# Conditioning products of a decoder step taken in batches: each tile loaded by a fixed pattern of granules, and two to four of them multiplied together behind a given projection matmul

## The chip, the cores and the metric

The kernel runs on one core of a Trainium2 chip. The metric is the device time of one execution in microseconds (us); three runs of the kernel before are known, and one profiled execution. The engines are called PE (matrix multiply), ACT, DVE and POOL (elementwise work); SP issues most of the DMAs, POOL and ACT some.

## The reference

One inference step of a decoder layer for 256 prompt tokens and 8 x 4 sample tokens, 288 columns in all, at a model width of 2048. Cut to what matters here:

```python
mod = jax.nn.silu(c) @ P['w_ada'] + P['b_ada']          # c: 9 rows; w_ada: 2048 x 12288
sh1, sc1, gt1, sh2, sc2, gt2 = split(mod, 6)
xn = rmsnorm(x, P['g_norm1']) * (1.0 + sc1) + sh1
mix, st = mixer(xn, ...)     # x @ w_in; RG-LRU, GLA and mLSTM branches; three gated merges; @ w_out
x = x + gt1 * mix
xn = rmsnorm(x, P['g_norm2']) * (1.0 + sc2) + sh2
x = x + gt2 * (jnp.square(jax.nn.relu(xn @ P['w_ff1'])) @ P['w_ff2'])
y = rmsnorm(x, g_final)
```

All values are 32-bit floats. The conditioning matrix `w_ada` alone is 100 MB, read once; it is multiplied with only nine rows (one prompt, eight samples).

## The kernel before, in words

**Projections.** Activations lie feature by feature: 16 tiles of 128 features by 288 columns. Weights come in granules: `stream` (L144) loads a granule of 256 rows by 512 columns (512 KB, L153), splits it into a rounded part `hi` on ACT (L154) and a rest `lo` on DVE (L155), and PE multiplies, for four blocks of 128 columns and two of 128 rows, `hi` with the high part of the activations, `hi` with their low part, and `lo` with the high part (L161 to L163). A granule is 24 matmuls. A projection over 2048 rows takes eight granules and ends with four evacuations (`evac`), each under high priority. Load and split are traced under high priority too, except in a few first blocks (`ahead`). The tiles `raw`, `hi` and `lo` have three buffers each; from the third merge on, `at` lets some of them use other memory in rotation (the tag `st`, which before holds recurrent states, and the slots 8 and 9).

**Conditioning.** `cond_product` (L204) multiplies the nine rows with one large matrix. A unit is a tile of 1 MB (768 KB in the correction product): one 128-row slice of 2048 columns, or two slices of 1024. Its four matmuls per slice (L216) go to the four 32-column parts of the PE array and add up in the PSUM tile `pa`. After 16 slices the sum is transposed and finished on DVE. The matrices follow in a fixed order: the two halves of SC1, then SH1, then the correction of the projections q, k, v for the shift ("cor", which reads `win` again), then GT1, SH2, SC2, GT2. From the second half of SC1 on this is the generator `fillers`. `run` asks it for one step after a granule as `pace["every"]` says: after each granule in the first blocks, then every second, two of three, every eighth. One step traces the load of a unit and its matmuls, at normal priority. `drain` runs the steps on until a given matrix is done. Each load gets its tile from `raw_tile`: the slots in `slots["ids"]` in turn (memory that lies free at the time), or the one ring tile `ag` (None). From the GLA branch on this is `ag` alone, until the output projection adds slots 8 and 9.

**Order.** The instructions are not executed in the order of the program text. A planner orders each engine's queue ahead of time, by a simulated timeline: among the instructions whose inputs and buffers it takes to be ready it picks by priority, which is the program's order, moved ahead for what stands under `tc.high_priority()`. Each engine then executes its queue in that order and waits where something is not there yet.

**Stages.** The first half of the scale, then q, k and half of v over the first and second halves of the features; the shift; the rest of v; two LRU blocks; the LRU branch; a small projection and the gates' two blocks; the GLA branch; the first merge, the mLSTM input and branch, the second and the third merge; the output projection; the second norm; then for eight blocks of the hidden layer `ff1` and `ff2`.

Of the kernel before, what the change touches and what calls it, by code (L numbers as in the profile page):

```python
# [8 lines left out]
F32 = mybir.dt.float32  # L9
# [19 lines left out]
CONSTS = [("ident", 128), ("eye", 32), ("bcol", 8), ("smask", 32), ("slo", 32), ("shi", 32),  # L29
          ("glo", 128), ("ghi", 128), ("causal", 128), ("bdm", 128), ("hsel", 4), ("seli", 128), ("self", 128), ("head", 4), ("half", 2)]  # L30
# [22 lines left out]
def trunk(ctx, tc, io):  # L53
# [92 lines left out]
    def stream(w, blk, act, kt, evac, g0=0, width=512, ahead=True, k0=0):  # L146
# [3 lines left out]
        for g in range(k0 // 2, kt // 2):  # L150
# [5 lines left out]
            for m in range(nm_t):  # L156
                for kk in range(2):
# [5 lines left out]
                    T.matmul(pss[m][:, :N], lo[:, kk, ms], xh, start=False, stop=k == kt - 1)  # L163
# [5 lines left out]
    pace = {"every": (), "n": 0}  # L169
# [26 lines left out]
    slots = {"ids": (None,), "n": 0}  # L196
# [8 lines left out]
    def cond_product(load, each, cols, stat, finish):  # L205


        ps = pa.tile([P, 512], F32, tag="pa", name=nm("pa"))
        for q in range(KT // each):
            raw = raw_tile()  # L210
            load(raw, q)
            for i in range(each):
                k = each * q + i
                v = raw[:, cols * i:cols * i + cols].rearrange("p (m j f) -> p j m f", j=4, f=32)
                for j in range(4):
                    T.matmul(ps[32 * j:32 * j + 32, 0:cols // 4], stat(k), v[:, j], start=k == 0, stop=k == KT - 1)  # L216
            if q < KT // each - 1:
                yield
        with tc.high_priority():
            for h in range(-(-cols // 1024)):  # L220
                finish(h, by_feature(ps, h, min(256, cols // 4 - 256 * h)))
        yield
# [15 lines left out]
    def ada(kind):  # L238
        def load(raw, k):
            Q.dma_start(raw.rearrange("p (h m) -> p h m", h=2), wada[kind, :, k].rearrange("h p m -> p h m"))  # L240
        return cond_product(load, 1, 2048, silu_c, ada_finish(kind))
# [1041 lines left out]
```

## Time and profile before

| | us |
|---|---|
| median of three runs | 2048.25 |
| lowest, highest | 2047.21, 2050.35 |
| the profiled execution | 2049.13 |
| its span, from the first to the last instruction | 2047.4 |
| PE busy | 1991.3 (97%) |
| DVE, ACT, POOL busy | 1030.3, 803.1, 304.0 |
| bytes moved by DMA | 429.69 MB, mean 210 GB/s |

The profile lists the instructions of that execution by line, engine and tiles, with their busy time and mean duration, and behind a bar the time that the engine stood idle before them and what ended it. The granted clock of PE is a share of full speed. PE's ends are modelled, since its matmuls are pipelined; so the starts of matmuls that follow one another are read rather than their durations.

### The profile page before, as it was taken

How to read it: one execution, taken by the hardware profiler on the slowest of the kernel's cores; microseconds unless marked ns; L12 is line 12 of the kernel's file. 1: busy time of each engine (PE TensorE's matmuls, PEld its weight loads, DVE VectorE, ACT ScalarE, POOL GpSimd, SP SyncE). 2: the span in 40 equal slices, each digit the busy share in tenths (PEclk: the TensorE clock that was granted, in tenths of full speed). 3: DMA queues.
4: the chain of work that ended last, by engine and by line, in shares of the span. 5: the costliest groups of instructions: out<-in, count | busy, mean ns of one | idle time of the engine just before them, and what ended most of it. 6: DMA issues, size and time to landing. Idle time of an engine off the chain costs nothing.

```text
span 2047.4 us, 35126 instructions
## 1 busy us (share of the span) xinstructions
PE 1991.3 (97%) x14726; PEld 1832.7 (90%) x14726; DVE 1030.3 (50%) x1410; ACT 803.1 (39%) x1099; POOL 304.0 (15%) x345
## 2 busy tenths in 40 slices
PE   6999999999999999999999999999999999999997
PEld 3778868987889798889998889999999999999997
DVE  4454556455554356464444464434454444454565
ACT  3323375332445332243333354444343434343434
POOL 0120112022212223100002241101010101010102
PEclk8989999999999999999999999999999999999999
DMA  9987686458673257877778655555555555555552
GB/s 389 349 317 249 220 311 210 157 201 294 220 242 127 89 196 243 260 263 266 249 238 328 221 174 165 166 166 165 168 166 165 166 168 164 167 165 165 165 165 98
DMA packets 121023, 429.69 MB, mean 210 GB/s; under 512 B 11601, under 2 KB 13809, under 8 KB 120737
## 3 DMA queue, kind: packets, MB, share of 16 engines
q1 hardware_dynamic: 111728, 393.59, 57.0%
q0 software_dynamic: 7984, 29.14, 3.9%
q10 hardware_dynamic: 1152, 4.72, 0.6%
q8 instruction: 115, 1.88, 0.4%
q14 instruction: 44, 0.35, 0.1%
HBM read 410.59 MB, written 16.81 MB: 209 GB/s over the span
## 4 chain that ended last, share of the span: by engine, by line
PE 89%; DMA 5%; DVE 3%; issue 2%; ACT 1%; POOL 1%; DVEq 0%; SPq 0%; POOLq 0%; ACTq 0%
PE mm L161 27%; PE mm L163 26%; PE mm L162 26%; PE pa L216 5%; DMA st<-mC 2%; DMA raw<-win 1%; DVE lo L155 1%; DMA s<-wada 1%; DMA o_C_s<-st 1%; ACT hi L154 0%; PE px L948 0%; PE pi L993 0%; PE px L675 0%; DMA st<-gla 0%; PE px L566 0%
## 5 line engine op out<-in xcount | busy, mean ns | idle before, releaser
L155 DVE TENSOR_TENSOR lo<-raw,hi 128x1024 fp32r<-128x1024 f32 (+1 forms) x424 | 541.3, 1279 | 596.6 <-ACT hi L154 580.0
L154 ACT ACTIVATE hi<-raw 128x1024 fp32r<-128x1024 f32 (+1 forms) x424 | 442.7, 1046 | 792.4 <-PE mm L162 677.7
L161 PE MATMUL mm<-xh,hi 128*128 128x288 f32 x2168 | 648.2, 301 | 10.1 <-ACT xh L341 5.5
L162 PE MATMUL mm<-xl,hi 128*128 128x288 f32 x2168 | 642.4, 297 | 1.2 <-DVE xl L342 1.2
L163 PE MATMUL mm<-xh,lo 128*128 128x288 f32 x2168 | 632.6, 297 | 3.5 <-DVE lo L155 3.5
L161 PEld LDWEIGHTS mm<-xh,hi 128*128 128x128 f32 x2168 | 408.1, 189 | 67.0 <-issue 40.0
L163 PEld LDWEIGHTS mm<-xh,lo 128*128 128x128 f32 x2168 | 405.9, 189 | 13.4 <-DVE lo L155 5.6
L162 PEld LDWEIGHTS mm<-xl,hi 128*128 128x128 f32 x2168 | 409.6, 189 | 3.2 <-DVE xl L342 1.5
L162 PE MATMUL mm<-s,hi 128*128 128x288 f32 x1176 | 349.0, 297 | 0.0
L161 PE MATMUL mm<-s,hi 128*128 128x288 f32 x1176 | 348.3, 298 | 0.0
L163 PE MATMUL mm<-s,lo 128*128 128x288 f32 x1176 | 345.9, 296 | 0.0
L161 PEld LDWEIGHTS mm<-s,hi 128*128 128x128 f32 x1176 | 220.6, 188 | 13.0 <-issue 10.9
L163 PEld LDWEIGHTS mm<-s,lo 128*128 128x128 f32 x1176 | 220.9, 188 | 1.8 <-issue 1.2
L162 PEld LDWEIGHTS mm<-s,hi 128*128 128x128 f32 x1176 | 221.3, 188 | 1.1 <-issue 0.4
L1121 POOL TENSOR_TENSOR t<-t 128x288 f32<-128x288 f32 x64 | 62.6, 990 | 639.6 <-ACT t L1120 639.6
L161 PE MATMUL mm<-s,st 128*128 128x288 f32 x488 | 143.9, 296 | 0.0
L162 PE MATMUL mm<-s,st 128*128 128x288 f32 x488 | 143.3, 294 | 0.0
L154 ACT ACTIVATE st<-s 128x1024 fp32r<-128x1024 f32 x80 | 84.8, 1060 | 135.6 <-PE mm L162 86.9
L161 PE MATMUL mm<-xh,st 128*128 128x288 f32 x408 | 120.7, 298 | 0.7 <-DVE xl L1107 0.7
L162 PE MATMUL mm<-xl,st 128*128 128x288 f32 x408 | 120.3, 296 | 0.0
L161 PEld LDWEIGHTS mm<-s,st 128*128 128x128 f32 x488 | 91.7, 188 | 0.8 <-ACT t L296 0.8
L162 PEld LDWEIGHTS mm<-s,st 128*128 128x128 f32 x488 | 91.9, 188 | 0.0
(373 smaller groups left out, 2113.7 us busy)
## 6 DMA issues: line engine op xcount, KB each, us to landing
raw<-win SPq DMA_DIRECT2D x192, 512.0 KB, 4.4
raw<-wf SPq DMA_DIRECT2D x176, 512.0 KB, 3.3
ag<-wada SPq DMA_DIRECT2D x57, 1024.0 KB, 5.9
s<-wf SPq DMA_DIRECT2D x80, 512.0 KB, 3.5
s<-wada SPq DMA_DIRECT2D x39, 1024.0 KB, 8.5
raw<-wout SPq DMA_DIRECT2D x32, 512.0 KB, 4.3
s<-win SPq DMA_DIRECT2D x11, 768.0 KB, 6.4
st<-mC POOLq DMA_DIRECT2D x16, 514.0 KB, 5.1
```

Of the source, the lines that this page charges most:

```text
L154: S.activation(hi, raw, AF.Copy)
L155: V.tensor_tensor(out=lo, in0=raw, in1=hi.bitcast(F32), op=ALU.subtract)
L161: T.matmul(pss[m][:, :N], hi[:, kk, ms], xh, start=k == k0, stop=False)
L162: T.matmul(pss[m][:, :N], hi[:, kk, ms], xl, start=False, stop=False)
L163: T.matmul(pss[m][:, :N], lo[:, kk, ms], xh, start=False, stop=k == kt - 1)
L216: T.matmul(ps[32 * j:32 * j + 32, 0:cols // 4], stat(k), v[:, j], start=k == 0, stop=k == KT - 1)
L1121: G.tensor_tensor(out=r, in0=r, in1=r, op=ALU.mult)
```

## The change

Load and product of a conditioning unit come apart. `cond_product` now yields units: a name, a function that takes a tile and issues its load, a function that multiplies it, and for the last unit of a matrix a function that finishes. A pattern of letters, one per granule, says what follows a granule: L loads the next unit (`load_one`, under high priority), V multiplies all units that are loaded and not yet multiplied, up to the end of a matrix (`visit`, under high priority, and on PE not ahead of the granule's last matmul), X does both. The patterns are X up to the shift; `LLLL.V` up to the LRU branch, with eight tiles in turn (slots 5, 6, 7, `ag`, 0, 1, 3, 4); nothing in the small projection; `LLLL.V..` in the gates; `LL.V..` and from its third block on `L.V...` in the first merge; nothing in the mLSTM input, the second merge and the output gate; `LLL.V..` in the third merge; `LLLL.V..` in the output projection; and in the feed-forward, from the second hidden block on, a pattern of 21 granules with three loads and one visit. Where tiles of the tag `st` hold a unit, two of them hold half a unit each, and the load is two DMAs.

Four things go with it. The split tiles `hi` and `lo` no longer use `st` and slot 9. Four constant tables (`shi`, `ghi`, `seli`, `self`, 416 columns) are gone: the upper clamps use the negated lower tables, and two selectors are made by POOL from the identity. The matmul that adds the new tokens' part to a sample state's output comes behind the products of the first states in place of ahead of them. And the three units that were asked for between the output projection and the second norm are no longer placed there. The first block of q is now loaded ahead like the others.

The diff, cut to its core:

```diff
-                    T.matmul(pss[m][:, :N], lo[:, kk, ms], xh, start=False, stop=k == kt - 1)
+                    pace["last"] = T.matmul(pss[m][:, :N], lo[:, kk, ms], xh, start=False, stop=k == kt - 1)
...
+    def every(p):
+        pace.update(every=p, n=0)
     def run(gen):
         for _ in gen:
-            pace["n"] += 1
-            e = pace["every"]
-            if e and e[pace["n"] % len(e)]:
-                next(fill, None)
+            if pace["every"]:
+                step(pace["every"][pace["n"] % len(pace["every"])])
+                pace["n"] += 1
...
     def raw_tile():
+        i = slots["ids"][slots["n"] % len(slots["ids"])]
         slots["n"] += 1
-        i = slots["ids"][slots["n"] % len(slots["ids"])]
         if i is None:
-            return ring.tile([P, 2048], F32, tag="ag", name=nm("ag"))
-        return flat(slot(i))[:, 0:2048]
+            return [ring.tile([P, 2048], F32, tag="ag", name=nm("ag"))]
+        if i == "st":
+            return [sp.tile([P, 1028], F32, tag="st", name=nm("st"), bufs=2)[:, 0:1024] for _ in range(2)]
+        return [flat(slot(i))[:, 0:2048]]
...
+                for h, r in enumerate(raw):
+                    v = r[:, w * i:w * i + w].rearrange("p (m j f) -> p j m f", j=4, f=32)
+                    for j in range(4):
+                        T.matmul(ps[32 * j:32 * j + 32, h * w // 4:(h + 1) * w // 4], stat(k), v[:, j], start=k == 0 and h == 0,
+                                 stop=k == KT - 1, skip_group_check=True)
...
+        for q in range(n):
+            def ld(q=q):
+                raw = raw_tile()
+                load(raw, q)
+                return raw
+            yield name, ld, lambda raw, q=q: products(raw, q), end if q == n - 1 else None
...
-    def fillers():
-        yield from ada_half(SC1, 1)
+    def units():
+        yield from ada_half("sc0", SC1, 0)
+        yield from ada_half("sc", SC1, 1)
...
+    def load_one():
+        u = next(left, None)
+        if u:
+            held.append((u[0], u[1](), u[2], u[3]))
+    def visit():
+        while held:
+            name, raw, products, end = held.pop(0)
+            products(raw)
+            if end:
+                end()
+                done.add(name)
+                return
+    def step(c):
+        if c in "LX":
+            with tc.high_priority():
+                load_one()
+        if c in "VX":
+            with tc.high_priority(), tc.issue_after(pace["last"].ins):
+                visit()
+    def settle():
+        while held:
+            visit()
     def drain(n):
         while n not in done:
-            next(fill, None)
+            if not held:
+                with tc.high_priority():
+                    load_one()
+            visit()
...
-    pace["every"] = (1,)
+    every("X")
     for b in range(NPRE):
-        run(stream(win, B_Q + b, act1, 8, to_slot((qk, vv)[b // 2], 4 * (b % 2)), ahead=b > 0))
+        run(stream(win, B_Q + b, act1, 8, to_slot((qk, vv)[b // 2], 4 * (b % 2))))
...
-    pace["every"] = (1, 0)
-    slots["ids"] = 6, 7, None
+    every("LLLL.V")
+    slots.update(ids=(5, 6, 7, None, 0, 1, 3, 4), n=0)
...
+    drain("cor")
+    settle()
+    every("")
...
+    every("LLLL.V..")
+    slots.update(ids=(6, 7, "st", None), n=0)
     run(stream(win, B_GATE, act1, KT, gate_silu(0)))
...
-            V.tensor_tensor(out=am[:, t], in0=am[:, t], in1=C("ghi").unsqueeze(1).to_broadcast(bc), op=ALU.min)
+            V.scalar_tensor_tensor(am[:, t], C("glo").unsqueeze(1).to_broadcast(bc), -1.0, am[:, t], ALU.mult, ALU.min)
...
-            T.matmul(po[0:32, 0:256], asb[:, h], vs[:, 0:256], start=True, stop=False, skip_group_check=True)
...
+                if q == 0:
+                    T.matmul(po[0:32, 0:256], asb[:, h], vs[:, 0:256], start=False, stop=False, skip_group_check=True)
...
-    drain("cor")
-    slots["ids"] = None,
+    settle()
     ygla = gla()
...
+            if br == 0 and b == 2:
+                settle()
+                slots.update(ids=(None,), n=0)
+                every("L.V...")
...
-    pace["every"] = (1, 0, 0)
+    slots.update(ids=(None, 7), n=0)
+    every("LL.V..")
     merge(0, ylru, io["wbl"])
+    settle()
+    every("")
...
-        def gate_rows(sel):
+        def gate_rows(i):
             p = misc()
-            T.matmul(p[:, :N], C(sel), sm, start=True, stop=True)
+            sel = t288()[:, 0:P]
+            G.tensor_copy(sel.rearrange("p (h i) -> p h i", h=4), ident.rearrange("p (h i) -> p h i", h=4)[:, :, i:i + 1].to_broadcast([P, 4, 32]))
+            T.matmul(p[:, :N], sel, sm, start=True, stop=True)
...
-    at.update(lo=(None, None, "st"), hi=(None, None, "st"))
+    slots.update(ids=(None, 5, "st"), n=0)
+    every("LLL.V..")
...
-    slots["ids"] = 8, 9, None
+    settle()
+    slots.update(ids=(8, 9, None, "st"), n=0)
+    every("LLLL.V..")
...
-    for _ in range(3):
-        next(fill, None)
...
-    at.update(raw=(None, None, 8), lo=(None, None, 9, None, None, "st"))
+    at.update(raw=(None, None, 8))
+    slots.update(ids=(9, None, "st"), n=0)
+    every("L..L..L.." + "...V" + 8 * ".")
     for hb in range(8):
-        pace["every"] = (1, 0, 0, 0, 0, 0, 0, 0)
         hn = ff1(hb + 1) if hb < 7 else None
         if hb == 6:
-            all_of(fill)
+            drain(GT2)
```

More of the change, by code (lines that the diff above doesn't have):

```diff
@@ L212, in cond_product, with products @@
+    def cond_product(name, load, each, cols, stat, finish):
+        acc_ = []
+        def products(raw, q):
+            if not acc_:
+                acc_.append(pa.tile([P, 512], F32, tag="pa", name=nm("pa")))
+            ps = acc_[0]
+            w = cols // len(raw)
             for i in range(each):
                 k = each * q + i
-                v = raw[:, cols * i:cols * i + cols].rearrange("p (m j f) -> p j m f", j=4, f=32)
-                for j in range(4):
-                    T.matmul(ps[32 * j:32 * j + 32, 0:cols // 4], stat(k), v[:, j], start=k == 0, stop=k == KT - 1)
@@ L984, in mlstm @@
             r = slice(32 * h, 32 * h + 32)
-            T.matmul(po[0:32, 0:257], psb[:, h], vs, start=True, stop=False, skip_group_check=True)
             for q in range(4):
@@ L1085, in trunk @@
             drain(SC2)
-            pace["every"] = ()
+            settle()
+            every("")
             for i in range(3):
```

77 lines of the change are left out of this document (31 added, 46 removed).

## The prediction

> **What bounds the kernel now.** I read the page first, then the chain of waits, then stretches of the conditioning tile `pa`, then PE's order of time around single visits. The page and its groups:
>
> ```profile
> span 2047.4 us, 35126 instructions
> PE 1991.3 (97%) x14726; PEld 1832.7 (90%) x14726; DVE 1030.3 (50%) x1410; ACT 803.1 (39%) x1099; POOL 304.0 (15%) x345
> ...
> PE mm L161 27%; PE mm L163 26%; PE mm L162 26%; PE pa L216 5%; DMA st<-mC 2%; DMA raw<-win 1%; DVE lo L155 1%; DMA s<-wada 1%; DMA o_C_s<-st 1%; ACT hi L154 0%; PE px L948 0%; PE pi L993 0%; PE px L675 0%; DMA st<-gla 0%; PE px L566 0%
> ...
> L155 DVE TENSOR_TENSOR lo<-raw,hi 128x1024 fp32r<-128x1024 f32 (+1 forms) x424 | 541.3, 1279 | 596.6 <-ACT hi L154 580.0
> L154 ACT ACTIVATE hi<-raw 128x1024 fp32r<-128x1024 f32 (+1 forms) x424 | 442.7, 1046 | 792.4 <-PE mm L162 677.7
> ```
>
> PE is the bound nearly everywhere: three projection lines make 79% of the chain, and the splitting of weights (L154) idles mostly because PE has not yet given a buffer back, not because data is missing. The one other item of size on the chain is `pa` (L216), the conditioning products, with 5%. So what shortens the kernel is PE time. How much `pa` takes by stretch (the first number after the width is PE's busy time on this tile, with its records; two records are one fp32 matmul, eight a unit of work), and, in the last row, all of PE in the feed-forward:
>
> ```profile
> 136.00:256.00 120.00, 16.32 (x128) 3.29 (x128) 0.64 (x3) 0.96 0.71 228
> 256.00:345.00 89.00, 14.65 (x96) 2.26 (x96) 0.00 (x0) 1.00 0.79 286
> 345.00:620.00 275.00, 25.41 (x144) 3.62 (x144) 0.78 (x2) 1.00 0.63 215
> ...
> 850.00:1203.00 353.00, 34.47 (x242) 5.39 (x242) 1.55 (x4) 1.00 0.74 258
> 1203.00:1250.00 47.00, 4.05 (x30) 0.72 (x30) 0.00 (x0) 0.96 0.50 167
> ```
> ```profile
> 1250.00:2030.00 780.00, 780.00 (x5872) 780.00 (x5872) 382.00 (x487) 311.67 (x402) 68.49 (x71) 1.00 0.51 162
> ```
>
> The five add up to 94.9 us for 640 records: 16 units of the correction product ("cor", 384 columns) and 64 of 512 columns. In the feed-forward a projection matmul starts every 780/5872 = 0.133 us, without holes.
>
> Now the price of a visit, that is, of a run of `pa` matmuls between projection matmuls. One unit alone, then two units together, in PE's order of time (start, duration):
>
> ```profile
> 930.52 0.29 PE L163 MATMUL mm<-xh,lo 128*128 128x288 f32 x1
> 930.75 1.06 PE L216 MATMUL pa<-ag,silc 128*32 128x512 f32 x8
> 931.74 0.40 PE L161 MATMUL mm<-xh,hi 128*128 128x288 f32 x1
> 931.98 0.30 PE L162 MATMUL mm<-xl,hi 128*128 128x288 f32 x1
> ```
> ```profile
> 1117.57 0.29 PE L163 MATMUL mm<-s,lo 128*128 128x288 f32 x1
> 1117.79 1.06 PE L216 MATMUL pa<-s,silc 128*32 128x512 f32 x8
> 1118.68 1.04 PE L216 MATMUL pa<-ag,silc 128*32 128x512 f32 x8
> 1119.65 0.40 PE L161 MATMUL mm<-s,st 128*128 128x288 f32 x1
> ```
>
> Alone: from 930.52 to 931.98 are 1.46 us for two projection steps of 0.133 and the visit, so the visit costs 1.19. Two: 1117.57 to 1119.65 are 2.08; less one step, plus the 0.11 by which the first step afterwards is longer (0.24 for 0.133), 2.05. The second unit costs 0.855, so a visit has a fixed price of 1.19 - 0.855 = 0.335 us: PE starts late on both changes between 128*128 and 128*32. A cor unit is 384/512 of 0.855, 0.641.
>
> **The change part by part, and the sum.**
>
> Removed visits. From 136 us on I count 89 visits in PE's order of time, the first and the last of them in the next fence. Their units cost 94.9 us busy and 89 x (1.19 - 1.06) = 11.6 at the edges: 106.5. Some of it stands in holes that stay when it goes:
>
> ```profile
> 137.98 0.85 PE L216 MATMUL pa<-s,mod 128*32 128x384 f32 x8
> 141.22 0.61 PE L161 MATMUL mm<-xh,hi 128*128 128x288 f32 x1 [2.38 <-ACT hi L154]
> ```
> ```profile
> 305.36 1.06 PE L216 MATMUL pa<-ag,silc 128*32 128x512 f32 x8
> 308.65 0.40 PE L161 MATMUL mm<-xh,hi 128*128 128x288 f32 x1 [2.23 <-DVE s L519]
> ```
> ```profile
> 1203.68 0.29 PE L163 MATMUL mm<-s,lo 128*128 128x288 f32 x1
> ...
> 1205.75 0.75 PE L300 MATMUL pi<-t,ones 128*128 128x288 f32 x2
> ...
> 1210.89 1.06 PE L216 MATMUL pa<-ag,silc 128*32 128x512 f32 x8 [2.44 <-DMA ag<-wada]
> ...
> 1212.65 0.81 PE L161 MATMUL mm<-xh,st 128*128 128x288 f32 x2 [0.69 <-DVE xl L1107]
> ```
> ```profile
> 1239.85 1.07 PE L216 MATMUL pa<-ag,silc 128*32 128x512 f32 x8
> ```
>
> At 138 PE waits for the shifted input, at 305 for the recurrent branch's work on ACT and DVE, between 1203.7 and 1212.7 for the second norm. One, one, two and one unit run there for nothing: 0.98 + 1.19 + 2.05 + 1.19 = 5.4. So 101.1 us can go.
>
> Added visits. Counting the new patterns by hand: cor, four visits of four; gates, two of four; first merge, four of two and four of one; third merge, seven of three; output projection, three (four, three, five); feed-forward, four (three, three, three, two). That is 28 visits for the same 80 units: 16 x 0.641 + 4 x 0.335 = 11.6, and 64 x 0.855 + 24 x 0.335 = 62.8, together 74.4. Gain 101.1 - 74.4 = 26.7. Nothing hides these visits; PE is the bound wherever they are put.
>
> The stage before ("X", up to 136 us) keeps one unit a granule: 24 visits of 1.19. By my count of PE's order there are 20 now, some of two units, so it loses some of the fixed prices; I take 0.5, between 0 and 4 x 0.335.
>
> The `po` matmul of the sample states (L704, L985) moves behind the first state products. Now it is often a visit of its own:
>
> ```profile
> 803.65 0.62 PE L985 MATMUL pi<-vs,s 128*32 128x257 f32 x2
> ```
>
> Joined to the next group it saves a fixed price, 8 heads x 0.335 = 2.7 at most and nothing at least; I take 2.3. It also no longer waits ahead of a state's DMA, and only PE's own queue stands behind it.
>
> Loads. Each unit's DMA goes to SP with high priority in program order, where before it stood behind prefetched weights. It waits for its buffer, and weights queue behind it on SP. The cover is buffering: a granule lasts 24 x 0.133 = 3.2 us, a batch has four megabytes at most, and eight granules with their batch (29 us) move 8.4 MB, 290 GB/s, little more than the 286 that the row from 256 to 345 ends with. Nothing, then; without cover a granule that misses costs up to 3.2 us, once a batch. Fifteen units go into `st` as two DMAs each: more SP issues, off the path.
>
> Buffers and the recurrent branch. Slots 0, 1, 3, 4, 5 now hold cor units until the last of the LRU granules, so the convolution and the POOL queue's two loads for it start later. The branch's last scans, and the first use of its result:
>
> ```profile
> L499 DVE TENSOR_TENSOR_SCAN s<-s,s x4: 1328/1330/1357, 303.1 to 306.9; 128x576 f32<-128x576 f32 x4
> ```
> ```profile
> L763 DVE SCALAR_TENSOR_TENSOR s<-s,mm x16: 441/448/455, 385.9 to 559.4; 128x288 f32<-128x288 f32 x16
> ```
>
> There are 79 us between them, so the branch itself is covered; if that cover were gone, its delay would show whole. But its ACT and DVE work competes with the weight splits for a PE that has 12 units to do there now and 8, in two visits, after. The nearest row is the wait of 2.23 at 308.65: I take 2 us, from 0 to four such waits, 9.
>
> The head selectors become two POOL copies of 128x128 instead of constants. Nearest copy:
>
> ```profile
> L427 POOL COPY s<-s x2: 853/1026/1200, 247.7 to 619.3; 128x256 f32<-128x256 f32 x2
> ```
>
> Two of half that size are 1 us at the head of a chain that projection granules cover; 0.5, between 0 and 2. The clamps that compute instead of reading a constant are DVE work of the same shapes in the place of others, three instructions for three: nothing, covered by PE or not. The smaller constant tile saves 416 x 512 bytes of DMA, 0.2 MB: nothing.
>
> The clock. Where PE waits, the granted clock (the third number from the end) falls:
>
> ```profile
> 136.00:150.00 14.00, 9.66 (x51) 8.45 (x50) 13.76 (x18) 5.17 (x5) 10.28 (x7) 0.68 0.60 187
> ...
> 1213.00:1220.00 7.00, 7.00 (x44) 7.00 (x44) 6.06 (x16) 4.66 (x14) 4.27 (x13) 0.78 0.45 150
> ```
>
> At half clock, 0.68 over 14 us is 9.0 us and 0.78 over 7 us is 3.1 us of halved clock; they cost half of that, 4.5 and 1.5. The change takes three units out of the second hole. If that hole then earns the long period of the first, it costs 3.0 more; if not, nothing. I take half, 1.5. The Trainium skill (TensorE: Matmul & The Clock Gate, Why this matters for your kernels) says that no idle gap over some 3 us should stand between bursts of matmuls, since one idle window takes the clock back to half. By that rule, removing these fillers is wrong and the sum would end 1.5 higher; the trace agrees that holes and halved clocks go together.
>
> Sum: -26.7 - 2.3 + 0.5 + 2 + 0.5 + 1.5 = -24.5. The profiled execution took 2049.13 us, 1.73 beside its span; it becomes 2024.6. The median of the runs is 0.88 lower: 2024, 1.2% faster.
>
> **The rivals.**
>
> A: the batches do not hold together. The pin sets only the earliest place. If the planner thinks that a batch's later tiles land late, it puts projection matmuls between them, and 80 units cost 16 x 0.976 + 64 x 1.19 = 91.8 instead of 74.4: 2024 + 17 = 2041. For it: that is how the 89 visits came about. Against: the loads stand several granules ahead of their visit.
>
> B: slower. The weight splits lose their extra buffers: from the third merge on `hi`, and `lo` too, had further tiles in rotation; now there are three of each. The evacuations at a block's end:
>
> ```profile
> L1120 ACT ACTIVATE t<-mm 128x288 f32<-128x288 f32 x64 | 25.4, 399 | 4.6 <-PE mm L163 4.5
> ...
> L341 ACT ACTIVATE s<-t 128x288 fp32r<-128x288 f32 x64 | 28.2, 440 | 24.5 <-POOL t L1121 24.0
> ...
> L342 DVE TENSOR_TENSOR s<-t,s 128x288 fp32r<-128x288 f32 x64 | 34.3, 569 | 17.1 <-ACT s L341 16.8
> ```
> ```profile
> L766 DVE SCALAR_TENSOR_TENSOR t<-s,mm 128x288 f32<-128x288 f32 x16 | 6.8, 445 | 12.0 <-PE mm L163 12.0
> ...
> L771 DVE SCALAR_TENSOR_TENSOR s<-s,s 128x288 fp32r<-128x288 f32 x16 | 10.8, 702 | 0.9 <-ACT s L770 0.9
> ```
> ```profile
> PE mm L163 <- DVE lo L155: 3.5, 4, 2.0
> ```
>
> With three buffers a split has two granules, 6.4 us, and takes 1.05 + 1.28 = 2.3. If a block's four evacuations stand ahead of it one after another, a first feed-forward block needs 4 x (0.40 + 0.44 + 0.57) + 2.3 = 7.9, late by 1.5, in 16 blocks 24; a third-merge block, with an ACT copy of the same shape as L341's, 4 x (0.445 + 0.70 + 0.44) + 2.3 = 8.6, late by 2.2, in four blocks 9. That gives 2024 + 33 = 2057. It cancels the gain from 1.2 us a block on. Against: the stages up to the third merge run with three of each, and all waits of PE for `lo` in the run are 3.5 us, in four places.
>
> C: the holes close as well, because batches arrive before they are needed: the 5.4 us of free units, the 2 us of the recurrent branch and the clock's 1.5 come back, and the waits in the rows above, 2.38 + 2.23 + 2.44 + 0.69 = 7.7: 2024 - 17 = 2007. For it: the wait at 1210.89 is one for a conditioning DMA. Against: the others are waits for ACT and DVE.
>
> **How the numbers follow.** Forecast 0.58, its own range 2014 to 2036; A 0.13; B 0.20; C 0.09. The range 2004 to 2052 takes in A, C and B up to where it cancels the gain; beyond it lie most of B's worse half and a little below C, under 2 in 10. The bound between change and none is 0.2%, 4 us, about what this kernel's measurements can tell. Faster: 0.58 + 0.09 + 0.10 of A = 0.77; same: 0.03 of A and 0.03 of B; slower: 0.17 of B.
>
> **What would show it.** Right: some 28 visits after 136 us, of 16 to 40 records; `pa` busy there near 74; feed-forward again at 0.133 us a matmul. Wrong: visits of eight records with projections between (A); waits of PE for `hi` or `lo` at block ends after the third merge (B); a long halved clock after 1200. A longer recurrent branch that reaches its first use would make me wrong in a way that I count as covered.

## The result, and the profile after

The kernel became slower, by 1.1%: 2071.68 us in the median (2069.22 to 2074.55) against 2048.09 for the kernel before beside it, a ratio of 1.0114 with a 95% interval from 1.0096 to 1.0131. I had forecast 2024 us.

The page of the changed kernel begins, and its chain of waits reads:

```profile
span 2067.4 us, 35383 instructions
...
PE 1968.8 (95%) x14846; PEld 1844.8 (89%) x14846; DVE 1027.5 (50%) x1410; ACT 802.1 (39%) x1099; POOL 302.2 (15%) x347
...
PE mm L161 26%; PE mm L162 25%; PE mm L163 25%; PE pa L226 5%; DMA raw<-win 2%; DMA raw<-wout 1%; DMA st<-mC 1%; DMA t<-ct 1%; DMA st<-gla 1%; DVE lo L155 1%; DMA o_C_s<-st 1%; PE pi L405 1%; ACT hi L154 1%; DVE s L468 0%; DMA s<-wada 0%
```

PE does 22.5 us less (1991.3 before), as intended; yet the span is 20.0 us longer, so by this measure PE stands still 42.5 us more. The chain names new items: `t<-ct` and `pi`, both from the first 60 us, and a DVE line, L468, which is a convolution. First the part that went as forecast, the stretches of `pa` by the changed kernel's own stage ends (stretch, width, PE busy on `pa` with its records), and one visit of three units in PE's order of time:

```profile
156.00:276.00 120.00, 15.41 (x160) 4.38 (x160) 1.43 (x4) 0.96 0.69 235
276.00:345.00 69.00, 3.65 (x40) 1.20 (x40) 0.00 (x0) 0.88 0.50 174
345.00:640.00 295.00, 15.60 (x136) 3.50 (x136) 0.78 (x2) 0.99 0.58 202
850.00:1216.00 366.00, 30.86 (x344) 9.97 (x344) 1.56 (x4) 1.00 0.74 267
1216.00:1260.00 44.00, 0.00 (x0) 0.00 (x0) 0.00 (x0) 0.92 0.39 126
1260.00:2050.00 790.00, 10.29 (x112) 3.23 (x112) 0.77 (x2) 1.00 0.52 171
```
```profile
985.70 0.29 PE L163 MATMUL mm<-xh,lo 128*128 128x288 f32 x1
985.92 1.06 PE L226 MATMUL pa<-ag,silc 128*32 128x512 f32 x8
986.80 1.04 PE L226 MATMUL pa<-s,silc 128*32 128x512 f32 x8
987.66 1.05 PE L226 MATMUL pa<-st,silc 128*32 128x256 f32 x16
988.64 0.40 PE L161 MATMUL mm<-xh,hi 128*128 128x288 f32 x1
988.88 0.30 PE L162 MATMUL mm<-xl,hi 128*128 128x288 f32 x1
```

From 985.70 to 988.88 are 3.18 us, less two projection steps of 0.133: 2.91 us for three units. The forecast prices say 0.335 + 3 x 0.855 = 2.90. There are 30 visits, the 28 that I had counted and one unit of the output projection that comes in two halves by itself; all of them come to about 75 us, against 74.4 forecast. So neither the price nor the count is where I went wrong.

The time lies elsewhere. I counted the projection matmuls in PE's order of time; there are 12720 in each kernel, so equal numbers are equal work:

| from matmul to matmul | stage | before, us | after, us | difference |
|---|---|---|---|---|
| start to first | input, first scale | 39.3 | 63.0 | +23.7 |
| first to 600 | q, k, v | 123.1 | 118.1 | -5.0 |
| 600 to 1000 | shift, rest of v, LRU blocks | 61.3 | 64.1 | +2.8 |
| 1000 to 2000 | LRU blocks and branch, gates, GLA begins | 193.7 | 203.2 | +9.6 |
| 2000 to 5000 | GLA to the third merge | 551.0 | 522.5 | -28.5 |
| 5000 to 6500 | third merge, output projection | 225.4 | 230.9 | +5.5 |
| 6500 to last | second norm, feed-forward | 838.0 | 849.3 | +11.3 |

The differences sum to +19.4. They hold conditioning products that stand in other rows now, so they have to be read beside PE's busy time on `pa` between the same matmuls. Over all rows it falls from 131.1 to 107.4 us: the intended gain is there. Of the -28.5 us, 22.2 are such products (33.9 before, 11.8 after), and the rest is within what that stretch varies between executions (below). In the row from 1000 to 2000 `pa` falls from 22.7 to 18.6 while the row grows by 9.6, so some 14 us are lost there. In the last row 10.8 us are the units that now stand in the feed-forward, which the forecast had in it. So the start gives back as much as `pa` gains, and three further places have losses of their own.

**The start.** SP's issues in order of time of the changed kernel, the landing and the wait of its first small load, `ct`, and the same load before:

```profile
0.73 1.47 SPq L268 DMA_DIRECT2D s<-wada  x3
2.25 0.81 SPq L260 DMA_DIRECT2D st<-wada  x1
...
14.94 2.81 SPq L153 DMA_DIRECT2D raw<-win  x2
17.80 1.27 SPq L268 DMA_DIRECT2D s<-wada  x2
19.11 0.47 SPq L268 DMA_DIRECT2D ag<-wada  x1
21.26 0.57 SPq L260 DMA_DIRECT2D st<-wada  x1
22.53 0.57 SPq L183 DMA_DIRECT2D t<-ct  x1
```
```profile
DMA to landing us min/median/max: 14.3/14.3/14.3
...
PE pi L405 <- DVE t L185: 37.5, 1, 37.5
```
```profile
0.73 0.39 SPq L180 DMA_DIRECT2D t<-ct  x1
...
DMA to landing us min/median/max: 3.8/3.8/3.8
```

`ct` holds the nine conditioning rows, 74 KB. Its load stands first in the program, at normal priority. The conditioning loads and the first block's weights now have high priority, so the planner put them ahead of it on SP, with both halves (L260) of a unit of the gate stage that found `st` tiles free. `ct` is issued at 22.5 us instead of 0.7 and then needs 14.3 us to land behind all that data instead of 3.8. Everything of the first scale waits for it, and so do the squares of x (L405), which use the same pool of small tiles.

**The recurrent branch.** Two stretches of the changed kernel (PE, PEld, DVE, ACT and POOL busy, granted clock, DMA share, GB/s), and two of PE's waits over the whole execution (total, times, longest):

```profile
274.00:280.00 6.00, 0.70 (x2) 0.35 (x2) 6.00 (x16) 2.27 (x6) 1.84 (x4) 0.66 0.34 140
280.00:286.00 6.00, 3.14 (x11) 2.71 (x11) 6.00 (x15) 0.66 (x2) 2.11 (x3) 0.50 0.21 63
```
```profile
PE mm L163 <- DVE lo L155: 7.2, 2, 6.5
PE mm L161 <- DVE s L568: 6.5, 1, 6.5
```

DVE is full, with the finish of cor (its sum added to q, k and v) and the convolution one after another; the split of the next weights (L155) waits in its queue, and PE waits 6.5 us for the split, at 276 us, and then runs at half clock. The second wait of 6.5 us, at 327, is for a gate evacuation behind the branch's last scans on DVE. It is the wait for which I had taken 2.23.

**The second norm**, in PE's order of time:

```profile
1215.20 0.75 PE L346 MATMUL pi<-t,ones 128*128 128x288 f32 x2 [0.46 <-ACT t L342]
1220.15 1.33 PE L161 MATMUL mm<-xh,hi 128*128 128x288 f32 x4 [4.20 <-DVE xl L1168]
1221.28 0.44 PE L162 MATMUL mm<-xl,hi 128*128 128x288 f32 x1
1221.52 0.44 PE L163 MATMUL mm<-xh,lo 128*128 128x288 f32 x1
```

A wait of 4.20 us, and behind it steps of 0.24 us, half clock. Before, a unit ran in that gap, at 1210.89, and the wait ahead of the first of these matmuls was 0.69.

### The profile page after: what moved, and what is told of

It is laid out like the page before. It is cut to its first block, busy times and chain, and to the rows that moved or that the text cites. A ratio compares the mean times of both kernels' runs of the same rounds, so it can differ in the third digit from the quotient of the medians.

```text
span 2067.4 us, 35383 instructions
## 1 busy us (share of the span) xinstructions
PE 1968.8 (95%) x14846; PEld 1844.8 (89%) x14846; DVE 1027.5 (50%) x1410; ACT 802.1 (39%) x1099; POOL 302.2 (15%) x347
## 4 chain that ended last, share of the span: by engine, by line
PE 87%; DMA 7%; DVE 3%; issue 2%; ACT 1%; POOL 0%; DVEq 0%; SPq 0%; ACTq 0%; POOLq 0%
PE mm L161 26%; PE mm L162 25%; PE mm L163 25%; PE pa L226 5%; DMA raw<-win 2%; DMA raw<-wout 1%; DMA st<-mC 1%; DMA t<-ct 1%; DMA st<-gla 1%; DVE lo L155 1%; DMA o_C_s<-st 1%; PE pi L405 1%; ACT hi L154 1%; DVE s L468 0%; DMA s<-wada 0%
## 5 line engine op out<-in xcount | busy, mean ns | idle before, releaser
L155 DVE TENSOR_TENSOR lo<-raw,hi 128x1024 fp32r<-128x1024 f32 (+1 forms) x456 | 578.1, 1270 | 677.9 <-ACT hi L154 664.9
L161 PE MATMUL mm<-xh,hi 128*128 128x288 f32 x2576 | 768.7, 300 | 24.5 <-ACT xh L387 8.8
L162 PE MATMUL mm<-xl,hi 128*128 128x288 f32 x2576 | 765.7, 298 | 0.9 <-DVE xl L388 0.9
L163 PE MATMUL mm<-xh,lo 128*128 128x288 f32 x2576 | 757.8, 298 | 7.2 <-DVE lo L155 7.2
L161 PEld LDWEIGHTS mm<-xh,hi 128*128 128x128 f32 x2576 | 486.7, 189 | 55.5 <-issue 23.7
L163 PEld LDWEIGHTS mm<-xh,lo 128*128 128x128 f32 x2576 | 486.2, 190 | 11.7 <-DVE lo L155 7.7
L161 PE MATMUL mm<-s,hi 128*128 128x288 f32 x1664 | 491.7, 297 | 2.8 <-ACT hi L154 2.8
L162 PE MATMUL mm<-s,hi 128*128 128x288 f32 x1664 | 491.0, 296 | 0.0
L163 PE MATMUL mm<-s,lo 128*128 128x288 f32 x1664 | 479.1, 296 | 0.0
L161 PEld LDWEIGHTS mm<-s,hi 128*128 128x128 f32 x1664 | 312.7, 188 | 9.0 <-issue 5.4
L162 PEld LDWEIGHTS mm<-s,hi 128*128 128x128 f32 x1664 | 313.3, 188 | 1.8 <-issue 1.2
L163 PEld LDWEIGHTS mm<-s,lo 128*128 128x128 f32 x1664 | 309.3, 188 | 1.3 <-issue 0.8
L155 DVE TENSOR_TENSOR lo<-s,hi 128x1024 fp32r<-128x1024 f32 x80 | 98.0, 1225 | 113.4 <-ACT hi L154 113.4
L154 ACT ACTIVATE hi<-s 128x1024 fp32r<-128x1024 f32 x80 | 84.9, 1061 | 140.4 <-PE mm L162 139.7
L405 PE MATMUL pi<-t,ones 128*128 128x288 f32 x32 | 11.1, 485 | 37.5 <-DVE t L185 37.5
L405 PEld LDWEIGHTS pi<-t,ones 128*128 128x128 f32 x32 | 6.6, 222 | 41.4 <-ACT t L404 37.9
```

The costliest lines, as they stand in the source:

```text
L154: S.activation(hi, raw, AF.Copy)
L155: V.tensor_tensor(out=lo, in0=raw, in1=hi.bitcast(F32), op=ALU.subtract)
L161: T.matmul(pss[m][:, :N], hi[:, kk, ms], xh, start=k == k0, stop=False)
L162: T.matmul(pss[m][:, :N], hi[:, kk, ms], xl, start=False, stop=False)
L163: pace["last"] = T.matmul(pss[m][:, :N], lo[:, kk, ms], xh, start=False, stop=k == kt - 1)
L405: T.matmul(ps[:, :N], ones, sq, start=k == 0, stop=k == KT - 1)
```

## The experiments

Ratios are to the kernel before, timed beside each of them. The stage of the mLSTM states, whose states pass through DMA, differs by some 7 us from one profiled execution to another with the same instructions (from the 3000th to the 5000th matmul 354.5 us in the changed kernel, 361.5 in e1); so what happens in one place is read in the traces, and what it is worth from medians. The ratios are known to 0.13 to 0.28% either way; a difference of 0.3% between two of the runs is only just clear of that. A stop is read between the starts of the matmuls around it, less one step, and is some 0.15 us longer than PE's idle time in the rows.

**e1: the load of `ct` first**

```diff
-    Q.dma_start(ct, io["ct"])
+    with tc.high_priority():
+        Q.dma_start(ct, io["ct"])
```

> The changed kernel with one line different: the load of the conditioning rows (the tile t from ct) is traced under high priority, so that it stands first on SP again. Theory 'late input': in the changed kernel this 74 KB load went out at 22.5 us, behind some 10 MB of tiles, and landed at 36.8; everything up to the first projection matmul (63.0 us, before 39.3) waited for it. Then the first projection matmul comes at 40 to 46 us and the time falls by 17 to 23 us, to 2049 to 2055. Rival 'caught up': the stage up to 180 us is short of DMA anyway and the late start is made good there; then the time falls by less than 6 us.

Measured: 2052.61 us, ratio 1.0024 (1.0010 to 1.0037). The first projection matmul, one row each from before, after and e1:

```profile
39.30 1.09 PE L161 MATMUL mm<-xh,hi 128*128 128x288 f32 x3 [5.50 <-ACT xh L341]
```
```profile
62.97 1.33 PE L161 MATMUL mm<-xh,hi 128*128 128x288 f32 x4 [4.91 <-ACT xh L387]
```
```profile
44.28 1.09 PE L161 MATMUL mm<-xh,hi 128*128 128x288 f32 x3 [3.60 <-ACT xh L388]
```

From 1.0114 to 1.0024 is 0.90% of 2048, 18 us, and the first matmul is 18.7 us earlier. One line of the program that the change does not touch was worth most of the loss.

**e2: e1, and other memory for the cor units**

```diff
-    slots.update(ids=(5, 6, 7, None, 0, 1, 3, 4), n=0)
+    slots.update(ids=(6, 7, None, 0, 1, 3), n=0)
```

> As e1, and the correction's tiles stay out of slots 4 and 5, which the recurrent branch's convolution needs (six tiles in turn in place of eight). Theory 'slots': the convolution waited for the last correction visit (its first operation at 271.3 us, before 215.0), so that its DVE work fell on the splits of the small projection: the wait of 6.8 us for lo at 276, that of 2.1 at 273 and a halved clock of 10 us behind them go; 8 to 14 us below e1. Rival 'scans and evacuations': the waits of this stage come from DVE's order around the branch whatever the slots; within 4 us of e1.

Measured: 2054.29 us, 1.0018 (1.0003 to 1.0033); the same as e1. The convolution starts at 217 us instead of 250, and the longest stop there fell from 6.8 to 3.4 us; but in place of one other of 2.05 us there are three of 1.0 to 1.6, and the half clock stayed as long. That the convolution started late for want of its slots is not by itself what costs; this theory fell.

**e3: e1, with the units of a batch multiplied one a granule**

```diff
         if c in "VX":
+            quota[0] = len(held)
+        if quota[0] and held:
+            quota[0] -= 1
             with tc.high_priority(), tc.issue_after(pace["last"].ins):
-                visit()
+                visit(1)
```

> As e1, but a batch is multiplied one unit after each of the following granules in place of all units behind one granule: the loads and their pattern are the same. Theory 'fixed price': from the correction on there are about 80 visits for 28, 52 x 0.335 = 17 us more PE time; 13 to 20 us above e1. Rival 'holes': PE has so many holes by now that single units fall into them; less than 6 us above e1.

Measured: 2061.18 us, 1.0057 (1.0029 to 1.0085). Batches are worth 0.33%, 7 us, over single units. e3 has 74 visits for e1's 30, so the fixed prices alone would be 44 x 0.335 = 14.7. The difference is mostly waits that single units fill: at 304 us, where e1 stops for 6.5 us, e3 stops for 1.9 and 1.2 and the half clock behind it is gone. The first stop, in e3 at 257 us, stays at 6.8: the cor finish and the convolution stand where they stood.

**e4: the changed kernel with all conditioning loads at normal priority**

```diff
-            with tc.high_priority():
-                load_one()
+            load_one()
...
             if not held:
-                with tc.high_priority():
-                    load_one()
+                load_one()
```

> The changed kernel with the conditioning loads traced at normal priority (everything else, the batches and the pins too, as changed; the load of the conditioning rows untouched). Theory 'late input' with its cause, the priority of the loads: the rows' load stands ahead of the conditioning tiles again, the first projection matmul comes at 40 to 46 us, and weights no longer stand behind bursts of loads (the wait of 2.5 us at 235); 2042 to 2055. Rival 'loads too late': at normal priority tiles arrive after their visit is due and PE waits for them in the visits; above 2060.

Measured: 2059.68 us, 1.0046 (1.0024 to 1.0067). The first matmul comes at 41.1 us. But then the loads fall behind in the q, k, v stage: matmul 96 to 288 takes 44.4 us against 38.4 in e1, with DMA full and PE standing still in this stretch of e4:

```profile
80.00:90.00 10.00, 6.63 (x38) 5.18 (x36) 8.66 (x16) 5.25 (x7) 6.61 (x5) 0.83 1.02 408
```

So in this stretch high priority for the conditioning loads pays, and it is `ct` behind them that cost. Over the whole kernel e4 is 0.22% above e1, which the intervals do not separate.

**e5: e1, and the start as before**

```diff
-        run(stream(win, B_Q + b, act1, 8, to_slot(...)))
+        run(stream(win, B_Q + b, act1, 8, to_slot(...), ahead=b > 0))
...
-    slots.update(ids=(6, 7, "st", None), n=0)
+    slots.update(ids=(6, 7, None), n=0)
```

> Kernel: e1_ct_first with two more parts of the start put back: the weights of the first projection block at normal priority (only blocks 1 and 2 ahead), and the gate stage's conditioning loads without the small `st` buffers, so that no load of that stage is drawn to the start. Theory 'what stands ahead on SP': three weight granules and one half unit stand before the sixteen half units of sc0, 2.5 MB that the first product waits behind; the first projection matmul comes at 39 to 40 us (44.3 in e1, 39.3 before the change) and the span is 3 to 5 us shorter than e1's, a ratio to the kernel before of 0.998 to 1.000. Rival 'given back': the first matmul is early but the first block's weights are late in turn, and the 24th projection matmul and everything behind it stand where e1 has them (50 us): ratio 1.001 to 1.003, as e1.

Measured: 2046.39 us, 0.9995 (0.9982 to 1.0008): 0.29%, 5.9 us under e1. The first matmul is at 39.7 us, 4.6 ahead of e1. The lead is 2.8 us at the 1000th matmul and 5.6 at the 5000th (947.4 and 952.9 us). So part of the early start is given back, and since the edit also leaves the gate stage three tiles in turn instead of four, how much of the 5.9 is the start's stays open. Together e1 and e5 are worth 24 us, as much as the whole loss; 18 of them are the one load.

**e6: e1, with three units for the second norm**

```diff
             settle()
-            every("")
+            slots.update(ids=(8, 9, None), n=0)
+            every("L.L.L...")
...
     xl2 = big.tile([P, KT, N], F32R, tag="xl", name="xl2")
+    every("")
+    settle()
```

> Kernel: e1_ct_first with three units of GT2 loaded in the last output-projection block and multiplied, unpinned, in the wait of the second norm, where the kernel before has them. Theory 'free filler': the hole of 4.16 us on PE in the norm (2.40 and 0.84 in the kernel before) becomes 2 to 3 us, one batch of three (2.91 us) goes out of the feed-forward part, and the halved clock behind the norm (3.4 us of trace time) shortens or goes: 3 to 7 us less than e1. Rival 'the norm's chain is slowed': the three units add 2.9 us in the norm that its own chain on ACT, DVE and POOL does not hide; then it only moves 2.9 us and the time is that of e1.

Measured: 2050.84 us, 1.0018 (1.0004 to 1.0032), e1's. In e6's order of time the units ran ahead of the sum of squares, not in the wait, which stayed:

```profile
1193.86 1.04 PE L227 MATMUL pa<-ag,silc 128*32 128x512 f32 x8
1194.83 0.75 PE L356 MATMUL pi<-t,ones 128*128 128x288 f32 x2
...
1201.72 0.90 PE L161 MATMUL mm<-xh,hi 128*128 128x288 f32 x4 [4.20 <-DVE xl L1181]
```

That tells nothing on what they would be worth in it; e10 pins them there.

**e7: e1, with the recurrent stage paced as before**

```diff
-    every("LLLL.V")
-    slots.update(ids=(5, 6, 7, None, 0, 1, 3, 4), n=0)
+    every(".S")        # S: load one, multiply one if more than two are held
+    slots.update(ids=(6, 7, None), n=0)
...
-    drain("cor")
-    settle()
-    every("")
...
+    drain("cor")       # only ahead of the GLA branch
     settle()
+    every("")
     ygla = gla()
```

The patterns of the gates go as well.

> Kernel: e1_ct_first with the stage from the fourth q/k/v block to the second gate block paced as in the kernel before: one conditioning unit loaded and one multiplied behind every second granule, through the small projection too, and `cor` finished only ahead of the GLA branch, not ahead of the recurrent branch. Theory 'the units and the late cor finish cover the recurrent branch': the holes of 2.05, 6.77 and 6.51 us at 251, 254 and 304 us and the halved clock behind them (8.5 us at half, 4 to 5 us lost) go down to the kernel before's (about 5 us in all); 19 us less, while 16 cor units singly cost 15.6 instead of 11.7 us and 8 of GT1 9.5 instead of 7.5: 8 to 15 us less than e1, 2037 to 2045 us, ratio 0.994 to 0.998. Rival 'the branch sets its own pace': the holes come wherever the units stand, because DVE is behind with the convolution and the scans: 0 to 6 us more than e1.

Measured: 2044.40 us, 0.9987 (0.9971 to 1.0003): 0.37%, 7.6 us under e1. Two stretches of e1, and of e7:

```profile
256.00:262.00 6.00, 1.30 (x5) 1.30 (x6) 6.00 (x15) 0.00 (x0) 2.16 (x3) 0.50 0.00 0
...
304.00:310.00 6.00, 0.63 (x5) 0.39 (x3) 5.96 (x8) 0.46 (x1) 0.49 (x1) 0.94 0.82 331
```
```profile
256.00:262.00 6.00, 5.52 (x37) 3.38 (x38) 0.93 (x3) 3.25 (x6) 0.00 (x0) 1.00 0.94 302
...
304.00:310.00 6.00, 4.90 (x37) 4.67 (x36) 6.00 (x9) 2.22 (x2) 2.81 (x5) 1.00 0.63 218
```

The stops of 6.77 and 6.51 us became 2.05 and 2.41, with no half clock behind them. The gain is just under what I expected (8 to 15, which had the dearer single visits in it). The edit changes four things together: the visits, the slots, the cor finish and the gates' patterns. e12 takes the visits apart from the rest.

**e8: e1, with the loads of the output projection spread**

```diff
-    every("LLL.V..")       # third merge
+    every("LLL.V.")
...
-    every("LLLL.V..")      # output projection; l: a load at normal priority
+    every("..lll.V.")
```

> Kernel: e1_ct_first with three units a period of six granules (not seven) in the third merge, and three (not four) a period of eight in the output projection, their loads there at normal priority two granules later. Theory 'the burst starves the weights': from 1070 to 1090 us four conditioning loads of 1 MB, 2.3 MB of x and the weights fill the DMA engines (412 GB/s), a weight granule comes 9 us late and PE stops for 3.63 and 1.7 us at 1091 and runs at half clock behind it; spread out, the stop is under 1 us and the time 3 to 6 us less than e1. Rival 'x alone does it': the stop stays, and the time is e1's within 2 us.

Measured: 2051.15 us, 1.0023 (1.0009 to 1.0038), e1's. The stop stays, 3.4 us at 1095; ACT's wait for the late weights, in e1 and in e8:

```profile
ACT hi L154 <- DMA raw<-wout: 11.3, 3, 10.9
```
```profile
ACT hi L154 <- DMA raw<-wout: 10.9, 2, 10.7
```

Three loads a period instead of four do not change the rush: the second copy of x, 2.3 MB, comes at the same moment (whether x alone does it was not tried).

**e9: e1, with the fourth weight buffer back in the third merge and the output projection**

```diff
+    at.update(lo=(None, None, "st"), hi=(None, None, "st"))
-    slots.update(ids=(None, 5, "st"), n=0)
-    every("LLL.V..")
+    slots.update(ids=(None, 5), n=0)
+    every("LL.V.")
...
-    slots.update(ids=(8, 9, None, "st"), n=0)
-    every("LLLL.V..")
+    slots.update(ids=(8, 9, None), n=0)
+    every("LLL.V.")
...
-    at.update(raw=(None, None, 8))         # feed-forward
+    at.update(raw=(None, None, 8), lo=(None,), hi=(None,))
```

> Kernel: e1_ct_first with the fourth hi and lo weight buffer put back from the third merge to the end of the output projection (every third hi and lo tile in an `st` buffer, as in the kernel before); the units there then have two and three buffers, so two are multiplied a visit in the merge and three in the output projection. e8 spread the conditioning loads and the stop of 3.4 us at the start of the output projection stayed: there the first late raw granule is 10.9 us late on ACT, and three granules of split weights cover 9.6 us of products. Theory 'shallower weight buffers' (rival B of the prediction, at another place): a fourth granule covers 3.2 us more, the stop goes below 1 us and the half clock behind it goes; 4 to 5 us gained, 1 us lost on three more visits: 3 to 4 us less than e1, ratio to the kernel before 1.0000 to 1.0010. Rival 'the transfers are the bound': a deeper buffer only moves the stop a few granules, the time is e1's or 1 us more.

Measured: 2052.06 us, 1.0024 (1.0009 to 1.0040). By the trace the theory holds in its place; stretches of e1, then of e9:

```profile
1090.00:1094.00 4.00, 1.32 (x10) 1.08 (x9) 0.00 (x0) 0.33 (x1) 0.00 (x0) 1.00 0.93 373
1094.00:1098.00 4.00, 3.22 (x14) 3.22 (x15) 3.17 (x3) 2.85 (x3) 0.00 (x0) 0.57 0.31 96
```
```profile
1090.00:1094.00 4.00, 4.00 (x32) 4.00 (x32) 1.23 (x1) 1.06 (x1) 0.00 (x0) 1.00 1.02 412
1094.00:1098.00 4.00, 4.00 (x31) 3.85 (x29) 0.00 (x0) 0.00 (x0) 0.00 (x0) 1.00 1.02 419
```

The stop and the half clock are gone, and matmul 5000 to 6500 takes 226.6 us instead of 231.3. The median does not show these 4.7 us, and I expected 3 to 4 in it. In the profiled execution matmul 3000 to 5000 took 3.9 us longer, part of it the stage that varies and part the smaller batches of the third merge; how much is which stays open.

**e10: put together.** The edits of e1, e5, e7 and e9, and e6's units pinned behind the last matmul of the sum of squares:

```diff
-        T.matmul(ps[:, :N], ones, sq, start=k == KT - 4, stop=k == KT - 1)
+        pace["ss"] = T.matmul(ps[:, :N], ones, sq, start=k == KT - 4, stop=k == KT - 1)
...
+    every("")
+    with tc.high_priority(), tc.issue_after(pace["ss"].ins):
+        settle()
```

> Kernel: e1 (ct first), e5 (first block's weights at normal priority), e7 (single units and late cor finish in the recurrent stage), e9 (fourth weight buffers), and the three units of e6 in the second norm, now pinned behind the last matmul of the sum of squares. If the losses add as measured one by one (e5 5.9 us under e1, e7 7.5, e9 3 to 4, the units in the norm 3 to 4 when they lie in its hole): 20 to 21 us under e1, about 2031 us, between 2026 and 2037, ratio to the kernel before 0.989 to 0.994. If they cover one another (an earlier start is waited for later, as the first blocks' loads are), 10 us under e1: 2040 to 2043, ratio 0.996 to 0.998.

Measured: 2029.94 us (2029.44 to 2035.90), ratio 0.9914 (0.9894 to 0.9935): faster than both kernels, and as far under e1 as the parts add up to. It is not the change with a repaired start alone: in the recurrent stage it goes back to single units. The norm in e10:

```profile
1185.91 0.75 PE L358 MATMUL pi<-t,ones 128*128 128x288 f32 x2 [0.46 <-ACT t L354]
1186.59 1.92 PE L227 MATMUL pa<-s,silc 128*32 128x512 f32 x16
1188.33 1.04 PE L227 MATMUL pa<-ag,silc 128*32 128x512 f32 x8
1190.86 0.80 PE L161 MATMUL mm<-xh,st 128*128 128x288 f32 x4 [1.49 <-DVE xl L1182]
1191.49 0.30 PE L162 MATMUL mm<-xl,st 128*128 128x288 f32 x1
1191.63 0.30 PE L163 MATMUL mm<-xh,st 128*128 128x288 f32 x1
```

Three units run for nothing: the wait falls from 4.20 to 1.49, the end of the wait lies 4.95 us behind the last matmul of the sum as in the changed kernel (1185.91 to 1190.86; 1215.20 to 1220.15), and the next steps are 0.13, full clock.

**e11: e10, with e3's edit**

> Kernel: e10 with the units of a batch multiplied one a granule and not together; loads, order and buffers as in e10. This prices the batches alone, where nothing else is in the way. Theory 'every visit costs its 0.335 us': some 53 units outside the recurrent stage in 53 instead of about 24 visits, 29 x 0.335 = 9.7 us more than e10, less what falls into holes: 7 to 10 us more. Rival 'a visit fills holes': as in e3, part of it comes free: 3 to 6 us more than e10.

Measured: 2037.47 us, 0.9950 (0.9929 to 0.9970): 0.36%, 7.4 us over e10. From 156 us on it has 75 visits and e10 has 50; 25 x 0.335 = 8.4. Outside the recurrent stage a saved visit is paid nearly in full, as far as 0.36% can be told.

**e12: e10, with batches of three in the recurrent stage**

```diff
-    every(".S")
+    every("L.L.LV")
```

> Kernel: e10 with the recurrent stage's units multiplied three at a time (three loads and one visit in six granules, the same rate) and not singly; the cor finish stays ahead of the GLA branch. e7 changed both things, and this tells them apart. Theory 'only the late cor finish mattered': the convolution still starts ahead of the cor finish, so the stops of 6.8 us at 251 us and 6.5 us at 304 us do not come back; 24 units in 8 visits and not in 24 save up to 16 x 0.335 = 5.4 us: 2 to 5 us less than e10, ratio to the kernel before 0.9885 to 0.9905. Rival 'the single units filled the branch's waits': single stops of over 3 us and a halved clock come back between 245 and 320 us, and the time is 0 to 8 us above e10's, ratio 0.9915 to 0.9955.

Measured: 2041.55 us, 0.9970 (0.9956 to 0.9984): 11.5 us over e10, though it saves 11 visits. Stretches of e12 with stops and half clocks that e10 does not have:

```profile
262.00:268.00 6.00, 3.44 (x12) 3.16 (x13) 1.22 (x1) 3.14 (x6) 0.00 (x0) 0.72 0.86 343
...
298.00:304.00 6.00, 4.56 (x19) 4.56 (x20) 5.99 (x10) 1.54 (x5) 0.00 (x0) 0.54 0.55 167
```

Between 240 and 330 us PE waits 11.3 us in e12 and 6.4 in e10, and the clock is halved for 17.1 us in e12 and not at all in e10. That is 4.9 and 8.5 us of cost, less 3.7 for the saved visits, together 9.7 of the 11.5; so the single units filled waits. The stop of 6.8 us does not come back. The late cor finish alone is not shown to be the reason, since the convolution has its slots here too, and in e2 that by itself halved the stop.

My theory that only the cor finish mattered fell, and by the traces neither change gains alone. From the 600th to the 2000th matmul, with 30 units in each of these runs, e1 (batches, early finish) takes 262.3 us, e3 (singly, early finish) 264.1, e12 (batches, late finish) 261.7, and e7 and e10 (singly, late finish) 256.8 and 255.3. Only the two together gain. (The batches are of four in e1 and of three in e12, and the slots differ with the finish.)

## Why the prediction was wrong, step by step

The kernel took 48 us more than I had forecast. Half of it, 24, is the step on the loads, which overlooked the start. The recurrent stage is 7.6 more, the second norm and the output projection together some 9 (e10 against e1, less what e5 and e7 gave), and some 6 stay open.

- **Added and removed visits (-26.7).** The price and the count were right (2.91 for 2.90, 30 visits for 28, 75 us for 74.4), and the batches held together, so rival A did not happen. What was too small is the list of units that ran for nothing, 5.4 us: I took only those in front of a shown wait. e12 against e10 shows that in the recurrent stage single units keep waits from arising, so they stand in front of no wait in the profile; there batching costs 11.5 us where I had it gain. Outside it the gain is real (e11).
- **Loads ("Nothing, then").** This step failed, and it alone cost as much as the whole gain forecast. I asked what queues behind a unit's load in the steady state, weights, and did not go through SP's queue at the start, where the first load of the program is the one that all conditioning products need. It was worth 18 us (e1), and the first block's weights and the drawn-forward half unit, tried together, up to 5.9 more (e5): 24, where my cover argument gave none and, without cover, 3.2 a granule.
- **The recurrent branch (+2, 0 to 9).** The cover of 79 us for the branch's result held; nothing waited for the result. But the sentence behind it, that its DVE work competes with weight splits, was the step, and I sized it by a single wait of 2.23. e7 is 7.6 us under e1 in spite of 16 more visits of 0.335, so about 13 us were at stake, above the range.
- **The clock (+1.5, 0 to 3.0).** At the norm it came as forecast, 6.8 us of half clock for 3.4 before, which costs 1.7 more. But I looked only there. Leaving out start and end, half clock is granted for 41.0 us in the changed kernel and 17.1 before; half of the difference is 12 us. It overlaps the other items, since each stop brings its own. The Trainium skill (TensorE: Matmul & The Clock Gate, What's actually happening) describes a freely running window of some 3.4 us; the half-clock stretches here agree, 3.4, 6.8 or 10.2 us long.
- **Rival B, shallower weight buffers.** The mechanism exists, at another place than I gave it: not at each block's end (no wait of PE for `hi` or `lo` in the feed-forward) but once, when the output projection begins (e9, 4.7 us in the trace, which the median does not show).
- **Rival C** did not happen: holes opened instead of closing.
- **The X stage (+0.5)** came out better: matmul 1 to 600 takes 119.7 us in e1 against 123.1. **The `po` matmul and the selectors** were not tried alone.

Without the losses at the start, in the recurrent stage, in the norm and at the output projection, the kernel takes 2029.9 us (e10). The forecast of 2024 had 3.5 us for them, 2 for the recurrent branch and 1.5 for the clock.

## What to carry to other kernels

When a group of loads is raised in priority, list what stood ahead of them on the same queue in the first microseconds: a small load that everything needs must be raised with them. Units of independent work between matmuls have a price per visit, but they also keep PE busy while another engine catches up; batch them where PE alone is the bound and the profile has no other full engine; beside a branch that fills DVE, as here, try them single. Before removing a filler, look for the wait that it prevents, not only for the wait that it stands in.

## What the runs showed that I had not expected

- A 74 KB load took 3.8 us to land as the first of its queue and 14.3 us with some 10 MB issued ahead of it on the same queue within 22 us.
- Short stops are enough for half clock: in e12 PE waited 1.96 us (244.7 to 247.0 us) and then stepped by 0.24 us, while in e10 a wait of 2.25 us at 293 was followed by steps of 0.13. So a length alone does not tell. What tells is a fixed grid: in each of the 14 traces the clock changes only at steps of 3.41 us. Of the steps at full clock between 66 and 2030 us, all 80 in which PE was idle for more than 1.85 us were followed by half clock, none of the 7788 with less than 1.5 us, and 6 of the 16 between. The 1.96 us of e12 lay in one step; the 2.25 of e10 fell into two, as 1.30 and 0.95.
- Three units between the last matmul of the sum of squares and the norm's end are free (e10). Just ahead of the sum they are not: the wait of 4.20 us stayed behind them (e6).
